# A hybrid backbone layer on one core: a list of small products on 32x32 tiles, and the products for an empty state left out

## The chip, the cores and the metric

One Trainium2 chip, one of its cores. The metric is the device time of one run of the kernel, in microseconds; less is better. Shares and rows of the profile are from one execution that the hardware profiler recorded.

## What is computed

One layer over 256 latent tokens and 256 context tokens, model width 2048, all in float32. Two token mixers stand side by side after one common projection: the first branch (RWKV-7, 16 heads of 64, worked as 8 pairs, scanned in both directions) and the second branch (gated DeltaNet, 8 heads of 128, in both directions). Their outputs are gated, merged and projected; a SwiGLU network of hidden width 5632 follows. The context tokens come first in each scan, from an empty state, and the state that they leave starts the scan of the latent tokens. The part that matters here, cut from the reference (the second branch; the kernel works the first branch in chunks with the same kind of triangular inverse):

```python
lmat = jnp.where(strict, jnp.einsum('nbhik,nbhjk->nbhij', kb, kc) * decay, 0.0)
sol = lax.linalg.triangular_solve(lmat, rhs, left_side=True, lower=True, unit_diagonal=True)
u, wk = sol[..., :dv], sol[..., dv:]
def step(s, inp):
    qk_i, u_i, w_i, qd_i, kt_i, gl_i = inp
    v_new = u_i - jnp.einsum('bhck,bhkv->bhcv', w_i, s)
    o = jnp.einsum('bhck,bhkv->bhcv', qd_i, s) + jnp.einsum('bhcj,bhjv->bhcv', qk_i, v_new)
    s = s * gl_i[..., None, None] + jnp.einsum('bhck,bhcv->bhkv', kt_i, v_new)
    return s, o
s0b = jnp.zeros((bsz, GDN_HEADS, GDN_HEAD_DIM, GDN_HEAD_DIM), jnp.float32)
```

## The kernel before

Large projections (`gemm`, and `products` in the middle stage) split each float32 operand into a high and a low part and take three matmuls per 128-row slice; ScalarE writes the high part of the weights, VectorE the low part (tiles `whi`, `wlo`, result `mm`). Three stages follow each other. Up to about 240 us the modulation vectors and the normalised input are made. From about 240 to 1300 us the two branches run, woven with the projections that they need. From there to the end come the merge, the output projection and the SwiGLU network, which are projections one after another.

The middle stage is written as generators (`prepare`, `grams`, `inverse`, `values`, `scan` per pair of the first branch; `features`, `tokens`, `decays`, `head_grams`, `head_inverse`, `head_scan` per head of the second; `products` for the projections). Each yields its next operation, or a list of matmuls, and class `Weave` puts all of them into one fixed order when the program is built. It keeps a clock for every engine from costs of its own (class `Lane`; a matmul with at most 64 rows and columns is charged by its rows and width), takes the operation that can start first by these clocks, and settles ties by the ranks in `RANK`. A list of matmuls is handed out in groups of 32, and another piece of work may come in between two groups. What the planner thinks an operation costs thus decides the order on every engine and on the DMA queues; what it really costs decides the time.

`invert` inverts the triangular blocks of 64x64 of a pair or head. For the first branch it is called once for a pair with `nu = 16` units of two 64x64 blocks each (32 blocks in all: 2 heads, 2 directions, 8 chunks), for the second branch once for a head with `nu = 8`. The 16x16 blocks on the diagonal are inverted by substitution on VectorE, after a round trip through DRAM that lays each block out along one partition. Then two steps of matmuls go from 16 to 32 and from 32 to 64. The step from 16 to 32 takes two lists of products, both into one PSUM tile (`pi`, seen as `pv`): the first list makes the product of the off-diagonal block with the inverse, on 32x32 tiles (`fours` names the 32x32 blocks); VectorE masks it into `Qm`; the second list multiplies the transposed inverse `Tx` by `Qm`; VectorE and ScalarE copy the result back into `T0`. In the second list, pairs (`nu = 16`) and heads (`nu = 8`) take different forms. In the trace the first list is `pi<-arena` (pairs) and the second `pi<-arena,Tx`.

In a head of the second branch, `tokens` scales the transposed keys into `keg` and `kta` for both directions and the four blocks of 128 tokens. `head_scan` multiplies `keg` by the inverse `tf` into `NW` (negated by ScalarE on its way out of PSUM), and then walks through the blocks in the order `gorder`, [2, 3, 0, 1] forward and [3, 2, 1, 0] backward: `NW` times the state `St` is subtracted from the values in every block but the first (the state is empty there), and `kta` times the new values makes the next state in every block but the last.

Most operations of the middle stage are issued from one helper, so they all carry its line, L147; in the rows they are told apart by the tiles.

Of the kernel before, what the change touches and what calls it, by code (L numbers as in the profile page):

```python
# [11 lines left out]
F32 = mybir.dt.float32  # L12
F32R = mybir.dt.float32r
AF = mybir.ActivationFunctionType
# [4 lines left out]
P = 128  # L19
# [264 lines left out]
def emit(ctx: ExitStack, tc, A, out, dbg=None):  # L284
# [6 lines left out]
    e, v, s = Lane(E, 0.0, 0.0, 0.0), Lane(V, 0.07, 0.00104, LAT["own"], 0.13), Lane(S, 0.09, 0.00086, LAT["own"], 0.165)  # L291
# [130 lines left out]
    with tc.tile_pool(name="p0", bufs=1) as p0, \  # L422
# [31 lines left out]
        ps = pst(pa, "pa")  # L454
# [9 lines left out]
        ps = pst(pa, "pa")  # L464
# [59 lines left out]
        for part in range(NE + 1):  # L524
            if part < NE:
                ps = pst(pmm, "mm")
# [48 lines left out]
    def invert(pool, Lt, parts, nu, which, full, fill):  # L575
# [7 lines left out]
        late = 0.0 if nu == 16 else 1.2  # L583
# [52 lines left out]
        for d in range(2):  # L636
            yield v.scalar_tensor_tensor(Qm[:, us[d]], pv[:, 0, us[d]], low16[:, d:d + 1],
                                         eye16[:, d].unsqueeze(1).to_broadcast([P, h2, 16]), ALU.mult, ALU.add)
        if nu == 16:
            yield [e.matmul(pv[64 * h:64 * h + 64, 1, u], Tx[64 * h:64 * h + 64, u, :], Qm[64 * h:64 * h + 64, u, :],  # L640
                            start=True, stop=True) for u in range(nu) for h in range(2)]
        else:
            yield [e.matmul(pv[r, 1, u], Tx[r, u, b:b + 32], Qm[r, u, :], start=True, stop=True) for h, u, b, r in fours]
        for h in range(2):
# [521 lines left out]
    gs = Shared()  # L1166
# [113 lines left out]
    def tokens(h):  # L1280
# [17 lines left out]
        for d in range(2):  # L1298
            col = 8 * d + h
            yield v.tensor_mul(keg[:, d], p4, egc[:, :, col:col + 1].to_broadcast([P, 4, P]))  # L1300
            yield v.tensor_mul(kta[:, d], p4, eta[:, :, col:col + 1].to_broadcast([P, 4, P]))
        weave.release(pab)
# [89 lines left out]
    def head_scan(h):  # L1392
# [9 lines left out]

        NW = gs.tile([P, 2, 4, P], F32, tag="NW", name="NW")
        for d in range(2):
            ps = yield psb
            yield [e.matmul(ps[:, P * b:P * b + P], keg[:, d, b, :], tf[:, 4 * d + b, :], start=True, stop=True) for b in range(4)]
            yield s.activation(NW[:, d].rearrange("p b c -> p (b c)"), ps, AF.Identity, scale=-1.0)
            weave.release(psb)
# [4 lines left out]
        for n in range(4):  # L1413
            bs = (gorder[0][n], gorder[1][n])
            ps = yield psb
            yield [e.matmul(ps[:, P * d:P * d + P], tf[:, 4 * d + bs[d], :], vt[:, bs[d], :], start=True, stop=n == 0) if i == 0 else
                   e.matmul(ps[:, P * d:P * d + P], NW[:, d, bs[d], :], St[:, d, :], start=False, stop=True)
                   for d in range(2) for i in range(1 + (n > 0))]
# [385 lines left out]
```

## Time and profile before

| | |
|---|---|
| time, median of 3 runs | 2226.66 us (2222.66 to 2231.06) |
| profiled execution, first to last instruction | 2220.3 us |
| TensorE busy | 2147.7 us (97%), 22780 matmuls |
| weight loads of TensorE | 1915.3 us (86%) |
| VectorE busy | 1554.6 us (70%) |
| ScalarE busy | 1063.0 us (48%) |
| GpSimd busy | 94.4 us (4%) |
| DMA | 435.13 MB, mean 196 GB/s |

Engines are named PE (TensorE's matmuls), PEld (its weight loads), DVE (VectorE), ACT (ScalarE), POOL (GpSimd) and SP (SyncE, which issues DMAs). Busy time is the union of what the engine had under way; matmuls overlap, so in a list of short ones the time from the list's start to the next operation's start is its price, not the length of one. A float32 matmul outside the split projections is recorded as two matmuls and two loads. "issue" in a wait means that the engine waited for nothing that the profile shows. Granted clock 1.00 is 2.4 GHz, 0.5 is 1.2 GHz; a mean between them is a mixture over the stretch.

### The profile page before, as it was taken

How to read it: one execution, taken by the hardware profiler on the slowest of the kernel's cores; microseconds unless marked ns; L12 is line 12 of the kernel's file. 1: busy time of each engine (PE TensorE's matmuls, PEld its weight loads, DVE VectorE, ACT ScalarE, POOL GpSimd, SP SyncE). 2: the span in 40 equal slices, each digit the busy share in tenths (PEclk: the TensorE clock that was granted, in tenths of full speed). 3: DMA queues.
4: the chain of work that ended last, by engine and by line, in shares of the span. 5: the costliest groups of instructions: out<-in, count | busy, mean ns of one | idle time of the engine just before them, and what ended most of it. 6: DMA issues, size and time to landing. Idle time of an engine off the chain costs nothing.

```text
span 2220.3 us, 54391 instructions
## 1 busy us (share of the span) xinstructions
PE 2147.7 (97%) x22780; PEld 1915.3 (86%) x22780; DVE 1554.6 (70%) x3244; ACT 1063.0 (48%) x1872; POOL 94.4 (4%) x171
## 2 busy tenths in 40 slices
PE   6998999999999999999999999999999999999998
PEld 4776688777778778878789899999999999999997
DVE  3457488778788668899998879956665665544454
ACT  3246555444555555545455465544444444444443
POOL 0000000000000011011110010100000000000000
PEclk8999999999999999999999999999999999999999
DMA  9965544344343446565667797927777776566665
GB/s 382 413 183 172 171 116 131 103 104 114 94 124 112 113 138 197 160 182 180 172 197 252 259 342 269 357 94 227 235 237 236 234 236 203 188 186 190 188 189 160
DMA packets 234484, 435.13 MB, mean 196 GB/s; under 512 B 115328, under 2 KB 129664, under 8 KB 229888
## 3 DMA queue, kind: packets, MB, share of 16 engines
q1 hardware_dynamic: 206304, 355.11, 50.9%
q0 software_dynamic: 14112, 51.39, 7.1%
q10 hardware_dynamic: 13824, 25.17, 3.4%
q8 instruction: 178, 2.92, 0.5%
q14 instruction: 66, 0.54, 0.1%
HBM read 405.76 MB, written 25.84 MB: 194 GB/s over the span
## 4 chain that ended last, share of the span: by engine, by line
issue 43%; PE 40%; DVE 8%; DMA 5%; ACT 2%; POOL 1%; SPq 0%; POOLq 0%; ACTq 0%; DVEq 0%
PE mm L147 19%; PE s L147 4%; PE pa L147 4%; DVE arena L147 3%; PE mm L380 2%; PE pi L147 2%; PE mm L382 2%; PE mm L381 2%; DVE wlo L147 2%; PE mm L475 1%; DVE aw L147 1%; DMA wraw<-w_low 1%; DMA wraw<-pa 1%; DMA aw<-ada_rest 1%; DMA arena<-scr 1%
## 5 line engine op out<-in xcount | busy, mean ns | idle before, releaser
L371 DVE TENSOR_TENSOR wlo<-wraw,whi 128x1024 fp32r<-128x1024 f32 x328 | 392.6, 1198 | 318.7 <-ACT whi L370 316.2
L370 ACT CAST whi<-wraw 128x1024 fp32r<-128x1024 f32 x328 | 336.6, 1028 | 457.8 <-PE mm L381 397.7
L147 PE MATMUL mm<-hxh,whi 128*128 128x256 f32 (+1 forms) x1376 | 465.6, 338 | 4.3 <-ACT whi L147 2.4
L147 PE MATMUL mm<-hxh,wlo 128*128 128x256 f32 (+1 forms) x1376 | 463.3, 337 | 4.6 <-DVE wlo L147 4.5
L147 PE MATMUL mm<-hxl,whi 128*128 128x256 f32 (+1 forms) x1376 | 462.4, 336 | 0.9 <-issue 0.9
L382 PE MATMUL mm<-hfh,wlo 128*128 128x256 f32 x1344 | 375.3, 279 | 0.2 <-DVE wlo L371 0.2
L380 PE MATMUL mm<-hfh,whi 128*128 128x256 f32 x1344 | 375.0, 279 | 0.0
L381 PE MATMUL mm<-hfl,whi 128*128 128x256 f32 x1344 | 375.0, 279 | 0.0
L147 PEld LDWEIGHTS mm<-hxh,wlo 128*128 128x128 f32 x1376 | 263.6, 192 | 31.5 <-DVE wlo L147 6.7
L147 PEld LDWEIGHTS mm<-hxh,whi 128*128 128x128 f32 x1376 | 263.4, 191 | 29.1 <-ACT whi L147 2.9
L147 PEld LDWEIGHTS mm<-hxl,whi 128*128 128x128 f32 x1376 | 263.3, 191 | 24.9 <-issue 4.2
L147 DVE TENSOR_TENSOR wlo<-wraw,whi 128x512 fp32r<-128x512 f32 x344 | 236.4, 689 | 50.8 <-ACT whi L147 48.4
L382 PEld LDWEIGHTS mm<-hfh,wlo 128*128 128x128 f32 x1344 | 252.8, 188 | 0.7 <-DVE wlo L371 0.6
L380 PEld LDWEIGHTS mm<-hfh,whi 128*128 128x128 f32 x1344 | 252.8, 188 | 0.0
L381 PEld LDWEIGHTS mm<-hfl,whi 128*128 128x128 f32 x1344 | 252.8, 188 | 0.0
L147 ACT CAST whi<-wraw 128x512 fp32r<-128x512 f32 x344 | 205.5, 617 | 85.0 <-PE mm L147 56.8
L147 DVE TENSOR_TENSOR arena<-arena 128x28 f32<-128x28 f32 (+13 forms) x538 | 131.4, 246 | 23.2 <-DMA arena<-scr 10.2
L380 PE MATMUL mm<-za,whi 128*128 128x256 f32 x512 | 142.9, 279 | 0.0
L381 PE MATMUL mm<-za,whi 128*128 128x256 f32 x512 | 142.7, 279 | 0.0
L382 PE MATMUL mm<-za,wlo 128*128 128x256 f32 x512 | 142.7, 279 | 0.0
L147 ACT ACTIVATE arena<-arena 128x512 f32<-128x512 f32 (+3 forms) x132 | 76.6, 593 | 45.6 <-DVE arena L147 33.9
L380 PEld LDWEIGHTS mm<-za,whi 128*128 128x128 f32 x512 | 96.3, 188 | 0.0
(325 smaller groups left out, 3892.7 us busy)
## 6 DMA issues: line engine op xcount, KB each, us to landing
wraw<-w SPq DMA_DIRECT2D x172, 512.0 KB, 4.2
wraw<-wgu SPq DMA_DIRECT2D x168, 512.0 KB, 4.6
aw<-ada_rest POOLq DMA_DIRECT2D x96, 512.0 KB, 5.4
aw<-ada_first SPq DMA_DIRECT2D x32, 1024.0 KB, 12.3
wraw<-wdn SPq DMA_DIRECT2D x64, 448.0 KB, 3.5
wraw<-wout SPq DMA_DIRECT2D x32, 512.0 KB, 6.8
aw<-ada_gt ACTq DMA_DIRECT2D x64, 256.0 KB, 5.0
wraw<-wdn SPq DMA_DIRECT2D x32, 512.0 KB, 3.6
```

The source lines that it names most:

```text
L147: return Op(self, cost, lambda: getattr(self.engine, name)(out, *a, **k), kind)
L370: S.copy(hi[:, c, :M], raw[:, c, :M])
L371: V.tensor_sub(lo[:, c, :M], raw[:, c, :M], hi[:, c, :M].bitcast(F32))
L380: E.matmul(ps, hi, Xh[:, k, :n], start=first and i == 0, stop=False)
L381: E.matmul(ps, hi, Xl[:, k, :n], start=False, stop=False)
L382: E.matmul(ps, lo, Xh[:, k, :n], start=False, stop=last and i == len(wt) - 1)
L475: E.matmul(ps[32 * g:32 * g + 32, 0:P], ckr[:, k].rearrange("p a b -> p (a b)"), aws[e, c][:, i, g], start=k == 0, stop=k == KT - 1)
```

## The change

Two edits in the middle stage. In `invert`, the pairs' second list takes the form that the heads' has: 64 products on 32x32 blocks in place of 32 products on 64x64 blocks. The off-diagonal 32x32 blocks, which the 64-row form multiplied along, are no longer read; the result that is copied back is the same. In the heads, the block that meets the empty state gets no `NW`: three products for a direction in place of four, `NW` holds three blocks in the order in which the scan takes them, and the negation covers 384 columns in place of 512. In `tokens`, for the backward direction the blocks of `keg` and `kta` that nobody reads are left out (block 3 of `keg`, block 0 of `kta`); for the forward direction the multiplies stay whole.

```diff
--- before.py
+++ after.py
@@ -636,11 +636,7 @@
         for d in range(2):
             yield v.scalar_tensor_tensor(Qm[:, us[d]], pv[:, 0, us[d]], low16[:, d:d + 1],
                                          eye16[:, d].unsqueeze(1).to_broadcast([P, h2, 16]), ALU.mult, ALU.add)
-        if nu == 16:
-            yield [e.matmul(pv[64 * h:64 * h + 64, 1, u], Tx[64 * h:64 * h + 64, u, :], Qm[64 * h:64 * h + 64, u, :],
-                            start=True, stop=True) for u in range(nu) for h in range(2)]
-        else:
-            yield [e.matmul(pv[r, 1, u], Tx[r, u, b:b + 32], Qm[r, u, :], start=True, stop=True) for h, u, b, r in fours]
+        yield [e.matmul(pv[r, 1, u], Tx[r, u, b:b + 32], Qm[r, u, :], start=True, stop=True) for h, u, b, r in fours]
         for h in range(2):
             yield [(s.copy if h else v.tensor_copy)(T0[r, us[d], b + 16 * d:b + 16 * d + 16], pv[r, 1, us[d]])
                    for d in range(2) for b in (0, 32) for r in (slice(64 * h + b, 64 * h + b + 32),)]
@@ -1297,8 +1293,9 @@
         p4 = ps.rearrange("p (b c) -> p b c", b=4)
         for d in range(2):
             col = 8 * d + h
-            yield v.tensor_mul(keg[:, d], p4, egc[:, :, col:col + 1].to_broadcast([P, 4, P]))
-            yield v.tensor_mul(kta[:, d], p4, eta[:, :, col:col + 1].to_broadcast([P, 4, P]))
+            late, soon = (slice(0, 4 - d), slice(d, 4))
+            yield v.tensor_mul(keg[:, d, late], p4[:, late], egc[:, late, col:col + 1].to_broadcast([P, 4 - d, P]))
+            yield v.tensor_mul(kta[:, d, soon], p4[:, soon], eta[:, soon, col:col + 1].to_broadcast([P, 4 - d, P]))
         weave.release(pab)
         weave.ready("tok", h)
 
@@ -1400,11 +1397,12 @@
             yield "out", NPAIR - 1
         tf, keg, kta, vt, Qe, PT = (o[n] for n in ("tf", "keg", "kta", "vt", "Qe", "PT"))
 
-        NW = gs.tile([P, 2, 4, P], F32, tag="NW", name="NW")
+        NW = gs.tile([P, 2, 3, P], F32, tag="NW", name="NW")
         for d in range(2):
             ps = yield psb
-            yield [e.matmul(ps[:, P * b:P * b + P], keg[:, d, b, :], tf[:, 4 * d + b, :], start=True, stop=True) for b in range(4)]
-            yield s.activation(NW[:, d].rearrange("p b c -> p (b c)"), ps, AF.Identity, scale=-1.0)
+            yield [e.matmul(ps[:, P * i:P * i + P], keg[:, d, b, :], tf[:, 4 * d + b, :], start=True, stop=True)
+                   for i, b in enumerate(gorder[d][1:])]
+            yield s.activation(NW[:, d].rearrange("p b c -> p (b c)"), ps[:, :3 * P], AF.Identity, scale=-1.0)
             weave.release(psb)
         if h:
             yield "gout", h - 1
@@ -1414,7 +1412,7 @@
             bs = (gorder[0][n], gorder[1][n])
             ps = yield psb
             yield [e.matmul(ps[:, P * d:P * d + P], tf[:, 4 * d + bs[d], :], vt[:, bs[d], :], start=True, stop=n == 0) if i == 0 else
-                   e.matmul(ps[:, P * d:P * d + P], NW[:, d, bs[d], :], St[:, d, :], start=False, stop=True)
+                   e.matmul(ps[:, P * d:P * d + P], NW[:, d, n - 1, :], St[:, d, :], start=False, stop=True)
                    for d in range(2) for i in range(1 + (n > 0))]
             Vn = gs.tile([P, 2, P], F32, tag="Vn", name="Vn")
             for d in range(2):
```

## Rows read from the trace of the kernel before

**Rows 1.** the page's busy time, share of the span and instructions of each engine
```profile
PE 2147.7 (97%) x22780; PEld 1915.3 (86%) x22780; DVE 1554.6 (70%) x3244; ACT 1063.0 (48%) x1872; POOL 94.4 (4%) x171
```

**Rows 2.** busy us in stretches of 50 us: start:end length, engines, clock, DMA
```profile
500.00:550.00 50.00, 49.78 (x669) 38.98 (x667) 44.44 (x115) 24.44 (x57) 2.31 (x6) 1.00 0.44 112
...
1100.00:1150.00 50.00, 49.98 (x532) 43.93 (x532) 48.69 (x130) 26.39 (x54) 4.88 (x8) 1.00 0.67 199
```

**Rows 3.** whom TensorE waited for, 240 to 800 us: total, times, longest
```profile
PE pi L147 <- issue: 7.5, 6, 2.8
```

**Rows 4.** TensorE's timeline, sixth inversion: start us, us, operation, count, idle before
```profile
626.50 1.26 PE L147 MATMUL pi<-arena 32*32 32x16 f32 x128
627.69 0.50 PE L147 MATMUL mm<-hxh,whi 128*128 128x512 f32 x1
...
629.51 2.08 PE L147 MATMUL pi<-arena,Tx 64*64 64x16 f32 x64
631.53 0.50 PE L147 MATMUL mm<-hxl,whi 128*128 128x512 f32 x1
```

**Rows 5.** the page's DMA queues: packets, MB, share of 16 engines
```profile
q8 instruction: 178, 2.92, 0.5%
```

**Rows 6.** busy us (x instructions), from one stall's end to the next
```profile
250.91:341.05 90.14, 89.77 (x1144) 73.75 (x1143) 73.42 (x175) 47.68 (x109) 2.76 (x8) 0.96 0.41 119
341.05:410.25 69.21, 66.00 (x1017) 53.51 (x1018) 57.40 (x144) 31.44 (x73) 3.50 (x6) 0.98 0.43 117
```

**Rows 7.** the same, from one instruction packet to the next, second, third, sixth inversion
```profile
337.04:341.05 4.01, 3.74 (x153) 2.94 (x140) 4.01 (x9) 1.51 (x4) 0.45 (x2) 1.00 0.62 210
404.39:410.25 5.86, 3.04 (x144) 2.33 (x137) 3.00 (x7) 0.00 (x0) 0.00 (x0) 1.00 0.64 206
...
626.95:630.88 3.94, 3.94 (x149) 3.33 (x140) 3.88 (x11) 0.00 (x0) 0.00 (x0) 1.00 0.70 207
```

**Rows 8.** TensorE's timeline, third inversion
```profile
406.32 1.11 PE L147 MATMUL pi<-arena 32*32 32x16 f32 x110
410.26 0.33 PE L147 MATMUL pi<-arena 32*32 32x16 f32 x18 [2.83 <-issue]
...
411.98 3.60 PE L147 MATMUL pi<-arena,Tx 64*64 64x16 f32 x64
415.51 1.22 PE L147 MATMUL pa<-Y,C 128*128 128x256 f32 x2
```

**Rows 9.** TensorE's timeline, fourth inversion
```profile
484.41 1.26 PE L147 MATMUL pi<-arena 32*32 32x16 f32 x128
...
487.45 1.22 PE L147 MATMUL pi<-arena,Tx 64*64 64x16 f32 x35
490.41 1.65 PE L147 MATMUL pi<-arena,Tx 64*64 64x16 f32 x29 [1.74 <-issue]
```

**Rows 10.** busy us and granted clock around the second, third and sixth inversion
```profile
340.00:350.00 10.00, 9.81 (x178) 7.65 (x178) 7.68 (x15) 3.36 (x8) 0.00 (x0) 0.83 0.28 90
410.00:420.00 10.00, 9.74 (x102) 8.08 (x102) 6.03 (x15) 5.81 (x16) 0.00 (x0) 0.66 0.11 34
...
628.00:634.00 6.00, 6.00 (x84) 5.01 (x83) 5.33 (x17) 1.45 (x5) 0.00 (x0) 1.00 0.44 137
```

**Rows 11.** TensorE's timeline, a head's second list at the lower clock
```profile
1083.53 1.04 PE L147 MATMUL pi<-arena,Tx 32*32 32x16 f32 x64
1084.49 0.71 PE L147 MATMUL pa<-arena 128*128 128x128 f32 x4
```

**Rows 12.** whom TensorE's weight loads waited for, 800 to 1260 us
```profile
PEld pi L147 <- DVE arena L147: 8.1, 11, 1.7
```

**Rows 13.** the chain that ended last, first head's NW products
```profile
887.90 0.89 PE s L147 x8
```

**Rows 14.** instructions by line and shape: busy us, mean ns, idle before
```profile
L147 DVE TENSOR_TENSOR arena<-pa,C 128x256 f32<-128x256 f32 x32 | 13.3, 417 | 5.9 <-PE pa L147 5.4
...
L147 DVE TENSOR_TENSOR keg<-pa,egc 128x512 f32<-128x512 f32 x16 | 10.8, 676 | 1.4 <-PE pa L147 1.4
```

## The prediction, made before the changed kernel ran

> **What bounds the kernel now.** I read the page's busy shares first, then the engines in stretches of 50 us. TensorE is busy for 97% of the span [rows 1]; in the stage of the first branch's heads (about 250 to 800 us) and in that of the second branch's (800 to 1260 us), where the two edits lie, it is all but full, and VectorE comes close only in the second [rows 2]. Then I read whom TensorE waited for between 240 and 800 us: the one large wait is "pi <- issue", 7.5 us in six pieces [rows 3]. So a microsecond of TensorE's own time there is nearly one of the kernel's, and its one large stall sits in the edited lists. Last, TensorE's timeline around an inversion.
>
> An undisturbed inversion, the sixth, looks like [rows 4]: the first list, 128 matmuls on 32x32 tiles (64 products, each recorded as two matmuls), runs from 626.50 to 627.69, which is 1.19 us, 9.3 ns each. Projections pass while VectorE masks the result. The second list, 64 matmuls on 64x64 tiles (32 products), runs from 629.51 to 631.53: 2.02 us, 31 ns each. The small form goes through three times as fast per matmul.
>
> **What the "issue" stalls are.** I counted instructions. Queue q8 carries them: 178 packets, 2.92 MB, so 16.4 KB each [rows 5]. TensorE has 22780 matmuls and 22780 loads [rows 1]: 256 to a packet. Between the end of one stall and the end of the next lie 2287 and, for the next pair, 2035 matmuls and loads [rows 6], 9 and 8 times 256 less 17 and 13 (semaphore instructions are not counted there). So TensorE stalls just where a new packet begins: it has used up 256 instructions before the next ones came. Going back 256 from each stall, the time from entering one packet to having the next is 4.01 us at the least and 5.86 us at the most in the inversions that stalled, and 3.94 us in the sixth, which did not stall [rows 7]. I take 5 us. Whoever issues 256 instructions faster than that waits; the first list is 256 instructions in 1.2 us. The third inversion stalls for 2.83 us in its first list [rows 8], the fourth for 1.74 us in its second [rows 9].
>
> **The change part by part.**
>
> *Second list.* Eight inversions each replace 64 matmuls on 64x64 tiles by 128 on 32x32 tiles, with the same 16 columns. The first list has that form, count and width, so its price is taken: 1.19 us for 2.02 us [rows 4], 0.83 us saved; seven times, 5.8 us. In the third inversion the list took 3.53 us [rows 8]: the granted clock over 410 to 420 us was 0.66 [rows 10], a part of it at 1.2 GHz. A 32x32 list of 64 there takes 0.96 us [rows 11], so 128 take 1.9 us, and 1.6 us is saved. Together 7.4 us; bounds 5.8 (the third gains nothing) and 9.0 (two more lists fall at 1.2 GHz, 0.8 us more each). It is TensorE's own time, on the path; the evictions behind it, on VectorE and ScalarE, only come earlier.
>
> Here a rule of the Trainium skill speaks against the change. The rows show 9.3 ns from one 32x32 matmul to the next [rows 4]. "TensorEngine Tiling (Array Packing)", section Performance Considerations, has every matmul carry an overhead of some 60 cycles however narrow it is, and warns against tiling where a dimension is already small; by that (an estimate: 60 cycles at 2.4 GHz, 25 ns) 64 more matmuls would cost 1.6 us an inversion, 12.8 us in all. The trace does not agree: its 9.3 ns lies far below.
>
> *Instructions.* 64 more matmuls bring 64 more loads: the second list issues 256 instructions in place of 128. The lists start 3.0 us apart in [rows 4] and in [rows 9]. The first list always holds one packet boundary. Now, the instruction 256 further on lies in the second list only if that boundary is in the first half of the first list; else the second list is over and slow 512-column matmuls are running. After the change it lies in the second list nearly always, and is reached as long after the first boundary as the lists are apart, 2.9 us. With 5 us to a packet that is a stall of 2.1 us. I let one in five escape (a boundary at the start of the first list, fetched while slow matmuls still run), and leave out two inversions of eight whose lists are far apart, as in [rows 8], 5.7 us: 6 x 2.1 x 0.8 = 10.1 us. Today's are 4.7 us (7.5 less the 2.83 of a first list). Added: 5.4 us. Bounds: 0 (packets come as in the sixth) and 12 (all eight stall by 2.1 us). In a stall only TensorE stands still; queued behind it are the projections, and what evicts them waits too.
>
> *Clock.* The granted clock falls around some inversions, to 0.83 of full over 340 to 350 us at the second, to 0.66 at the third, and stays at 1.00 at the sixth [rows 10]. In [rows 8] it was down after an issue stall between short matmuls. With shorter lists and longer stalls I see no net sign: 0. One such fall costs what the second's does, 0.17 of 10 us, 1.7 us; three falls more or two less give bounds of +5 and -3.5 us.
>
> *Order.* The order of all instructions between 240 and 1300 us comes from a planner in the file that uses its own costs. It charges the old second list 32 x (0.01 + 0.00075 x 16) = 0.70 us and the new one 64 x (0.01 + 0.00037 x 16) = 1.02 us. So the plan shifts by 0.3 us at each inversion, and everything after the first may interleave anew: casts, weight loads on SP's queue, evictions. No row prices that. TensorE's loads wait for VectorE in the second stage 8.1 us in eleven pieces [rows 12]; such waits may come or go. I take 0, bounds 5 us either way.
>
> *Heads of the second branch.* Per head and direction one 128x128x128 product (two matmuls) goes: four matmuls a head. Eight take 0.89 us [rows 13], 0.11 us each: 0.45 us a head, 3.6 us in all. On VectorE one keg and one kta multiply of each head shrink from 512 to 384 columns; 512 cost 676 ns and 256, also from PSUM, 417 [rows 14], so 0.13 us each, 2.1 us in 16; ScalarE's negation shrinks by a quarter. ScalarE idles enough to hide its part; TensorE's 3.6 us count. Bounds: 0 (VectorE, at 48.69 of 50 us [rows 2], holds the pace there) and 5 (its own part helps as well).
>
> **Sum.** -7.4 + 5.4 + 0 + 0 - 3.6 = -5.6 us. The profiled span is 2220.3 us, the median of the runs 2226.66; I leave the 6.4 us between them. 2226.66 - 5.6 = 2221 us. What is late next is TensorE as before, with its own instructions inside the inversions.
>
> **Rivals.** *Packets come in time.* The 5.4 us fall away: -11.0 us, 2215.7; with the better ends of lists and heads, -14, 2212.7. For it: the sixth inversion's 3.94 us [rows 7]. Against: the ones with 4.01 to 5.86. Chance 0.20.
>
> *Starved lists,* slower than before. All eight second lists stall by 2.1 us (16.8 in place of 4.7: +12.1), and the clock falls at three inversions more than now (+5); lists and heads give -11.0: +6.1, 2232.8. It decides from the point where stalls and falls add over 11 us, 1.4 us an inversion. For it: [rows 8] has stall and lower clock together. Against: the sixth has neither. Chance 0.13.
>
> *No faster per matmul.* If something else than the tile's size holds this list (its operands, its bank), a matmul still costs 31 ns: 128 take 4.0 us, +2.0 x 8 = +15.8, heads -3.6: +12.2, 2238.9. The change would then not do what it says. Against: the first list, with the same bank and width [rows 4]. Chance 0.04.
>
> *A new order outweighs the edit,* by some 10 us around the forecast: 2211 or 2231. Chance 0.11, half each way. The forecast itself: 0.52.
>
> **How the numbers follow.** A measurement of this kernel tells about 0.5% from no change, 11.1 us: faster is below 2215.5, slower above 2237.8. Faster: a little over half of the first rival (0.13), half of the new order (0.05), the low edge of the forecast (0.06): 0.24. Slower: the no-faster case (0.03), the upper end of starved lists and new order (0.07): 0.10. The rest, 0.66, can't be told from no change. The range for 8 in 10 reaches from the better half of the first rival, 2209 with the order's bound, to the starved lists, 2234.
>
> **What would show it.** In the profile after: "pi<-arena,Tx" as 128 matmuls on 32x32 tiles in about 1.2 us outside stalls, eight times; "pi <- issue" up from 7.5 to about 13 us; stalls still multiples of 256 instructions apart; "s<-TF,keg" with 96 matmuls. Wrong would be: issue stalls that stay or shrink, a list of 2 us without a stall, or a stage whose length moves against its lists.

## The result and the profile after

The changed kernel takes 2237.82 us (median of 5 runs, 2232.97 to 2239.14), the kernel before, run beside it, 2226.19 us: a ratio of 1.0045, 95% interval 1.0024 to 1.0067. It is 11.6 us slower, 10 us by the ratio. The forecast was 5.6 us faster, and the time lies above the range's upper end of 2234; it stays just within the 0.5% that was called no change. The profiled execution takes 2234.9 us, 14.6 more than that of before.

The page of the changed kernel, its span, its busy line and the queue of the instructions:

```profile
span 2234.9 us, 55358 instructions
...
PE 2146.3 (96%) x23260; PEld 1915.0 (86%) x23260; DVE 1557.2 (70%) x3244; ACT 1061.1 (47%) x1872; POOL 97.1 (4%) x171
...
q8 instruction: 182, 2.98, 0.6%
```

Against [rows 1] TensorE has 480 more matmuls (8 x 64 in the lists, less 32 in the heads), as the edit says, and nearly the same busy time. What grew is the time in which it is not busy: 2234.9 less 2146.3 is 88.6 us; before it was 72.6.

The lists themselves cost what was expected of them. TensorE's timeline of the changed kernel (start us, us, operation, count, idle before) at the fifth and the seventh inversion, both second lists on 32x32 tiles:

```profile
536.87 1.26 PE L147 MATMUL pi<-arena 32*32 32x16 f32 x128
540.48 1.23 PE L147 MATMUL pi<-arena,Tx 32*32 32x16 f32 x125
544.54 0.23 PE L147 MATMUL pi<-arena,Tx 32*32 32x16 f32 x3 [2.83 <-issue]
...
684.77 1.26 PE L147 MATMUL pi<-arena 32*32 32x16 f32 x128
687.87 1.59 PE L147 MATMUL pi<-arena,Tx 32*32 32x16 f32 x128
```

125 of them take 1.23 us, where 64 on 64x64 tiles took 2.02 us in [rows 4]; and the fifth stalls for 2.83 us just before its last three. In the changed kernel each of the eight second lists but the last has a wait in it, of 0.15 us (the seventh) to 2.83 us (the fifth); without it they take 1.1 to 1.5 us, and the last, at 1.2 GHz, 1.9. TensorE's waits from 240 to 800 us (total, times, longest), the row that answers to [rows 3] and the same wait in another tile:

```profile
PE pi L147 <- issue: 9.3, 7, 2.8
PE pa L147 <- issue: 1.3, 1, 1.3
```

Now the stages. Start:end and length, busy us of TensorE, its loads, VectorE, ScalarE and GpSimd (with instructions), granted clock, DMA. The bounds are the same events in both kernels: the first pair's first list, the last pair's first list, the first head's first list, the first gate product (`oah`) and the first output product (`mh`). Before:

```profile
246.80:754.60 507.80, 497.94 (x7297) 401.95 (x7298) 413.44 (x1038) 263.08 (x613) 15.47 (x41) 0.97 0.41 112
754.60:871.60 117.00, 116.37 (x1225) 97.32 (x1224) 87.36 (x202) 64.48 (x125) 11.63 (x15) 1.00 0.51 160
871.60:1263.10 391.50, 378.98 (x4336) 329.12 (x4335) 351.94 (x919) 198.13 (x400) 43.66 (x69) 0.99 0.63 193
1263.10:1368.50 105.40, 100.28 (x830) 98.23 (x829) 84.72 (x134) 59.58 (x82) 9.30 (x17) 1.00 0.88 315
```

After:

```profile
248.50:746.00 497.50, 487.02 (x7801) 397.50 (x7800) 418.08 (x1041) 263.21 (x613) 15.81 (x41) 0.99 0.43 117
746.00:874.00 128.00, 118.02 (x1203) 95.29 (x1204) 82.88 (x188) 62.46 (x123) 11.30 (x14) 0.91 0.41 126
874.00:1272.00 398.00, 379.56 (x4250) 330.53 (x4249) 348.88 (x920) 194.81 (x395) 46.45 (x69) 0.97 0.62 191
1272.00:1380.70 108.70, 105.50 (x911) 103.14 (x912) 89.16 (x144) 62.78 (x90) 8.72 (x16) 0.97 0.87 311
```

In the stage of the first branch's inversions, where the lists lie, the changed kernel is 10.3 us shorter. That is not the lists' doing: in before_neworder, a run that is told of below, the second lists are still on 64x64 tiles, the order is the changed kernel's, and the stretch is 11.6 us shorter than before, with 56 more matmuls in it:

```profile
245.60:741.80 496.20, 490.46 (x7353) 402.13 (x7352) 418.40 (x1041) 263.61 (x613) 15.83 (x41) 0.99 0.43 117
```

Nor does one execution settle a difference of some 5 us in such a stretch. In heads_oldorder, also told of below, every engine has the same instructions there in the same order as before, and the stretch takes 5.5 us less:

```profile
248.70:751.00 502.30, 493.00 (x7294) 397.97 (x7293) 413.65 (x1038) 262.66 (x614) 14.26 (x41) 0.98 0.41 113
```

The changed kernel gives 11.0 us back between the last inversion and the first head, where TensorE idles 10.0 us (0.6 before) and the clock is 0.91 (1.00 before); 6.5 more among the heads, 3.3 in the stage behind them. With 1.7 us ahead of the first list and 2.4 in the long last stage this makes the 14.6.

A clock of 0.91 over 128 us is a mean of stretches at 2.4 GHz (1.00) and at 1.2 GHz (0.50): 0.09 x 2 x 128 = 23 us were at the lower level. Over the whole span the mean clock is 0.983 before and 0.977 after, 75 and 103 us at 1.2 GHz. Where TensorE is the bound, each such microsecond does half a microsecond's work, so the 27 us more cost about 14.

What TensorE waited for in those 128 us:

```profile
PE mm L147 <- ACT whi L147: 4.2, 2, 2.8
PE mm L147 <- DVE wlo L147: 2.8, 2, 2.3
PE pi L147 <- issue: 1.7, 1, 1.7
PE pa L147 <- issue: 1.3, 1, 1.3
```

7.0 of the 10.0 us are waits for split weights, of which before had 0.2 us in that stretch. They come with the order: before_neworder, with the work of before, has 7.0 us of them too (742 to 865 us):

```profile
PE mm L147 <- ACT whi L147: 4.0, 2, 2.6
PE mm L147 <- DVE wlo L147: 3.0, 3, 2.3
```

One of them in the changed kernel, in the timeline of all engines:

```profile
819.25 1.14 ACT L147 CAST whi<-wraw 128x512 fp32r<-128x512 f32 x2
...
819.92 0.50 PE L147 MATMUL mm<-hxh,whi 128*128 128x512 f32 x1 [1.41 <-ACT whi L147]
...
820.35 0.74 DVE L147 SCALAR_TENSOR_TENSOR arena<-mm,PR,arena 128x510 f32<-128x510 f32 x1
821.01 0.68 DVE L147 TENSOR_TENSOR kta<-pa,eta 128x512 f32<-128x512 f32 x1
821.60 0.74 DVE L147 SCALAR_TENSOR_TENSOR arena<-mm,PR,arena 128x510 f32<-128x510 f32 x1
822.26 0.68 DVE L147 TENSOR_TENSOR wlo<-wraw,whi 128x512 fp32r<-128x512 f32 x1
...
823.00 0.80 PE L147 MATMUL mm<-hxh,wlo 128*128 128x512 f32 x1 [2.35 <-DVE wlo L147]
```

and the same place in stretches:

```profile
810.00:818.00 8.00, 8.00 (x36) 5.83 (x35) 2.61 (x7) 4.09 (x10) 2.66 (x4) 1.00 0.58 198
818.00:829.00 11.00, 7.25 (x24) 5.57 (x23) 9.13 (x18) 4.64 (x9) 0.53 (x1) 0.69 0.43 131
```

The high parts were written from 819.25 on, 0.57 us each; the low part of them stands behind three other multiplies in VectorE's order and is issued at 822.26. TensorE has nothing else next in its own order, waits 1.41 and 2.35 us, and runs at 1.2 GHz for a while (0.69 over the stretch). VectorE is busy for 9.1 of the 11 us; what TensorE needs next stands late in its order. That order is the planner's, and the planner was given new charges.

### The profile page after: what moved, and what is told of

It reads as the page before. It is cut to its first block, busy times and chain, and to the rows that moved or that the text cites. A ratio compares the mean times of both kernels' runs of the same rounds, so it can differ in the third digit from the quotient of the medians.

```text
span 2234.9 us, 55358 instructions
## 1 busy us (share of the span) xinstructions
PE 2146.3 (96%) x23260; PEld 1915.0 (86%) x23260; DVE 1557.2 (70%) x3244; ACT 1061.1 (47%) x1872; POOL 97.1 (4%) x171
## 5 line engine op out<-in xcount | busy, mean ns | idle before, releaser
L147 DVE TENSOR_TENSOR arena<-arena 128x512 f32<-128x512 f32 (+13 forms) x538 | 132.6, 248 | 20.0 <-DMA arena<-scr 5.1
```

The source lines that it names most:

```text
L147: return Op(self, cost, lambda: getattr(self.engine, name)(out, *a, **k), kind)
```

## The experiments

Two ways to hold things apart. In *the old order* the edited operations are issued, but the planner is charged what it was charged before, so that in the middle stage every engine's sequence is that of the kernel before except for the edited operations themselves. In *the new order* it is the other way round. The operations of the merge and of what follows are written behind the planner's stage, and the planner does not set their order. By the traces the runs in the old order keep the sequences of before up to 1268 us; behind that some differ from it in a few places. before_neworder has the changed kernel's sequence on TensorE, VectorE and ScalarE up to 1281 us (SyncE's DMAs differ in four places); behind that, in the merge, its order is a third one. All runs, each beside the kernel before, whose median was 2223.9 to 2226.2 in the five sessions ("not busy" is the profiled span less TensorE's busy time; the last two columns are of the profiled execution):

| run | us | ratio to before (95%) | not busy us | mean clock |
|---|---|---|---|---|
| before | 2226.19 | | 72.6 | 0.983 |
| changed kernel | 2237.82 | 1.0045 (1.0024 to 1.0067) | 88.6 | 0.977 |
| both_oldorder | 2228.38 | 1.0014 (0.9997 to 1.0032) | 81.5 | 0.982 |
| before_neworder | 2242.92 | 1.0078 (1.0055 to 1.0101) | 88.7 | 0.979 |
| list_only | 2225.56 | 1.0002 (0.9984 to 1.0019) | 85.2 | 0.984 |
| heads_only | 2251.77 | 1.0105 (1.0078 to 1.0132) | 92.9 | 0.977 |
| heads_oldorder | 2224.18 | 0.9999 (0.9984 to 1.0015) | 73.8 | 0.984 |
| list_oldorder | 2229.87 | 1.0021 (1.0003 to 1.0038) | 85.2 | 0.982 |
| after_headsold | 2229.70 | 1.0021 (1.0002 to 1.0040) | 87.2 | 0.984 |
| before_turn | 2261.04 | 1.0160 (1.0133 to 1.0187) | 92.4 | 0.980 |
| before_hop | 2266.46 | 1.0182 (1.0151 to 1.0212) | 106.4 | 0.975 |
| before_own | 2265.40 | 1.0176 (1.0136 to 1.0216) | 96.6 | 0.975 |
| after_own | 2244.42 | 1.0085 (1.0055 to 1.0114) | 95.9 | 0.980 |
| list_twice | 2264.24 | 1.0177 (1.0153 to 1.0200) | 98.5 | 0.978 |
| list_half | 2219.56 | 0.9978 (0.9963 to 0.9992) | 79.7 | 0.985 |
| first_big | 2216.18 | 0.9965 (0.9941 to 0.9988) | 69.2 | 0.990 |
| first_wide | 2222.53 | 0.9982 (0.9967 to 0.9998) | 77.0 | 0.992 |
| first_wide_heads | 2219.30 | 0.9970 (0.9956 to 0.9984) | 76.1 | 0.988 |

### Work and order apart

Both edits, charged as before (the heads' operations likewise, through a helper that sets an operation's charge back):

```diff
-            yield [e.matmul(pv[64 * h:64 * h + 64, 1, u], Tx[64 * h:64 * h + 64, u, :], Qm[64 * h:64 * h + 64, u, :],
+        ops = [e.matmul(pv[r, 1, u], Tx[r, u, b:b + 32], Qm[r, u, :], start=True, stop=True) for h, u, b, r in fours]
+        yield paired(ops) if nu == 16 else ops
```

(`paired` makes 32 operations of two products each, charged 0.022 us like the 64-row products.)

> Both edits of the change, but the planner charges the edited operations as it charged the old ones (32 entries of two products each at the old list's cost and kind, a fourth empty entry in each list of three NW products, old costs for the shortened multiplies and the negation), so that the order of the woven stage is that of the kernel before. Theory A, the new interleaving costs the time and the edited work itself is a gain: TensorE's waits on the heads' casts are as in the kernel before, the granted clock falls in the heads twice as before (10 us), and the time is 2215 to 2222 us, ratio 0.995 to 0.998. Theory B, the work itself costs it (twice the instructions in the second lists, so longer fetch stalls, and a lower clock after them): 'pi <- issue' rises from 7.5 to 13 us or more, the clock falls at more inversions, and the time is 2230 to 2240 us.

Measured: 2228.38 us, some 3 us above before and between what A (2215 to 2222) and B (2230 to 2240) gave; issue waits between 240 and 800 us are 12.3 us, close to B's sign. The same work in the changed kernel's order has the ratio 1.0045 in place of 1.0014: the order makes some 7 us of it, between 1 and 13 by the two intervals (an estimate). The work of the kernel before, in the order that the changed kernel's charges give:

```diff
+            yield [x for o in ops for x in (Op(e, 0.01 + 0.00037 * 16, o.call, (32, 32)), Op(e, 0.01 + 0.00037 * 16, lambda: None, (32, 32)))]
...
+            yield charged(v.tensor_mul(keg[:, d], p4, egc[:, :, col:col + 1].to_broadcast([P, 4, P])), 512, 512 - 128 * d)
```

> The work of the kernel before (32 products on 64x64 tiles, four NW blocks, full multiplies), but the planner charges it as it charges the changed kernel's, so that the woven stage has the changed kernel's order. Theory A: slower than the changed kernel by what the edited work saves, 5 to 11 us: 2243 to 2249 us. Theory B: about the time of the kernel before, 2222 to 2230 us, since the work that costs the time is gone.

Measured: 2242.92 us, a ratio of 1.0078, at A's lower end. Not one operation more or less, and the kernel is 17 us slower (0.0078 x 2224): an order alone can cost more than the changed kernel loses. But it is not the price of the changed kernel's order. Of the 20.5 us that the profiled execution takes more, 14.6 lie in the stage behind the heads, 120.0 us against 105.4 before and 108.7 in the changed kernel, where the order is a third one:

```profile
1267.50:1387.50 120.00, 108.32 (x915) 105.54 (x916) 92.47 (x146) 64.91 (x91) 9.79 (x18) 0.96 0.81 288
```

From the first list to the first head the two do have the same order. There before_neworder takes 618.6 us and the changed kernel 625.5 (before 624.8, heads_oldorder with the same work 621.1). So there the order itself loses nothing, and the edited lists lose some 7 us in it, by one execution each: issue waits are 10.6 us against 4.2, and 38 us against 24 are at 1.2 GHz from 240 to 875 us. Among the heads it is the other way: 403.3 us in before_neworder, 398.0 in the changed kernel, 391.5 before. Each edit alone, with its own charges: list_only is the first hunk of the change, heads_only the other three.

> The second list on 32x32 tiles alone, ordered by the planner with its own charge for it; the heads as before. Theory A: another order, whose cost or gain is not foreseen, within some 15 us of 2222 us. Theory B: the list is what costs: 2235 to 2242 us, the heads' edit having given 3 to 4 us back in the changed kernel.

> The heads' edit alone, planned as it comes; the second list on 64x64 tiles. The first branch has the order of the kernel before until the heads begin to be woven in. Theory A: an order of its own among the heads, within some 10 us of 2223 us. Theory B: 2222 to 2223 us, the edit's 3.6 us less.

Measured: 2225.56 and 2251.77; the second lies above what either theory gave for it. The list's edit is neutral with its own charges, the heads' costs 23 us (0.0105 x 2224), though it only leaves work out. The list's order is not harmless either. In list_only, from the first pair's list to the last pair's, and from there to the first head's:

```profile
248.80:742.10 493.30, 483.85 (x7805) 394.70 (x7807) 417.83 (x1041) 263.79 (x613) 15.83 (x41) 1.00 0.43 118
742.10:872.20 130.10, 119.11 (x1229) 96.81 (x1228) 87.60 (x201) 64.00 (x125) 12.47 (x15) 0.95 0.42 133
```

14.5 us are won in the first stretch and 13.1 lost in the second, on waits for `whi` and `wlo` (7.4 us) as in the changed kernel.

### Which edit, which charge

> The heads' edit alone, with the planner still charged the old cost for the shortened multiplies, the shortened negation and the product left out, so that all instructions come in the order of the kernel before. Theory A (the new order is what costs; the edited work itself is worth what the rows say): TensorE's own 0.45 us a head come out, 2220 to 2222.5 us beside 2224. Theory B (the heads' edit itself disturbs the second stage, by VectorE's or ScalarE's results coming at other times): 2230 to 2252, as the edit gave with its own plan (2251.8).

Measured: 2224.18 us, ratio 0.9999, some 2 us above A's range and far from B's. The 23 us of heads_only were the order's alone; the work left out is worth 1 us here, at most 3.6 by the interval. The NW products are 12 in place of 16 a head, and from the first head's to the last head's TensorE's busy time falls from 360.7 to 357.2 us, the 0.5 us a head that the prediction took; the stretch itself falls from 372.9 to 371.7 only.

> Both edits in full; the planner is charged the new cost for the second list, and the old cost for the heads' multiplies, negation and product. Theory A (the heads' new charges bring the order that costs): 2221 to 2226, the list's edit alone (2225.6) less 0 to 3.6 us for the heads. Theory D (the two edits together cost, whatever the order): 2234 to 2242, as the changed kernel.

Measured: 2229.70 us, between the two theories' numbers and 8 us under the changed kernel. With the heads charged as before most of the loss seems gone, but the intervals of the two (1.0002 to 1.0040 and 1.0024 to 1.0067) overlap.

> The list's edit alone (second list as 64 products on 32x32 tiles), with the planner charged the old cost for it, so that all instructions come in the order of the kernel before. Theory A (the edit saves TensorE 6 to 7 us and its longer stalls at packet boundaries and what is late next give 4 to 9 us back): 2221 to 2227 beside 2224, TensorE's busy time down by about 6 us and its waits up by as much. Theory L (in a held order the whole saving stays): 2216 to 2219.

Measured: 2229.87 us, above what A gave and 11 us above L: in a held order the list's edit costs 0.7 to 8.5 us. A part of the saving goes at the last inversion, which ran undisturbed before. TensorE's timeline there (the view ends at 758 us; 92 matmuls of the list stand behind the stall), and the granted clock behind it:

```profile
752.59 1.32 PE L147 MATMUL pi<-arena 32*32 32x16 f32 x128
...
755.36 0.49 PE L147 MATMUL pi<-arena,Tx 32*32 32x16 f32 x36
757.94 0.25 PE L147 MATMUL pi<-arena,Tx 32*32 32x16 f32 x5 [2.09 <-issue]
```

```profile
752.60:767.90 15.30, 13.21 (x290) 10.95 (x289) 5.90 (x18) 4.51 (x16) 1.05 (x1) 0.67 0.18 65
752.60:875.30 122.70, 120.04 (x1289) 100.17 (x1288) 87.49 (x202) 64.47 (x125) 11.58 (x15) 0.96 0.49 152
```

The new instructions bring a stall of 2.09 us in the second list, as the prediction had it, and behind it 10 us at 1.2 GHz (0.33 x 2 x 15.3). From the last list to the first head it takes 122.7 us, before 117.0. Up to that list it took 502.3 us against 507.8, but so did heads_oldorder with the lists of before, so that nothing shows the lists to have won there.

### How much an order is worth

The work of the kernel before, untouched, with one constant of the planner moved by 2 to 6%:

```diff
-LAT = dict(dma=2.04, hop=0.255, own=0.092, grp=32, cg=4, turn=0.17)
+LAT = dict(dma=2.04, hop=0.255, own=0.092, grp=32, cg=4, turn=0.18)
```

`turn` becomes 0.18 in before_turn; in before_hop it is `hop`, 0.26, and in before_own `own`, 0.095. after_own sets `own` to 0.095 in the changed kernel.

> All work is that of the kernel before; only one constant of the planner is changed, the time it puts in for a change of tile form on TensorE, 0.17 to 0.18 us. It plans another order of the same instructions. Theory A (the order alone moves the time by more than the edits are worth): off by 5 us or more from 2224, either way, up to 25 slower; the difference sits among the second branch's heads and in the stage behind them, with TensorE waits on casts and VectorE and a lower granted clock there. Theory C (only the particular charges for the heads give a bad order; neighbouring plans are alike): 2221 to 2227.

> All work is that of the kernel before; one other constant of the planner is changed, the time it puts in from one engine's result to another engine's start, 0.255 to 0.26 us. Theory A (plans of the same work spread by tens of us, and the plan of the kernel before is a good one among them): 2230 to 2262, with more TensorE waits and more low clock than before. Theory C (the turn's plan was an outlier): 2222 to 2229.

> All work is that of the kernel before; a third constant of the planner is changed, the time between two dependent instructions of VectorE, ScalarE or GpSimd, 0.092 to 0.095 us. Theory A (plans of the same work spread by tens of us, and the plan of the kernel before is a good one among them): 2230 to 2262. Theory C: 2222 to 2229.

> The changed kernel, both edits with their new charges, with the same third constant changed, 0.092 to 0.095 us: another order of the changed kernel's work. Theory A (the changed kernel's 2238 is one draw from a spread that the order makes, not the price of the edits): anywhere from 2215 to 2262, off from 2238 by 5 us or more. Theory D (the edits themselves cost 12 to 14 us): 2234 to 2242.

Measured: 2261.04, 2266.46 and 2265.40 us, 35 to 41 us slower than before for the same work, and 2244.42 for the changed kernel's. Theory A holds for the three, and its upper ends (25 us, and 2262) were too low (in before_turn 12 of the 32 us of the profiled execution lie ahead of the heads, where A did not put them); the particular charges of the heads are not special. For after_own the interval, 1.0055 to 1.0114, reaches the changed kernel's 1.0067, so that this run decides little. Four other orders of the work of before are 17 to 41 us slower, the two of the changed kernel 12 and 19. Only with the planner's constants and the heads' charges left alone did new orders come out near the old one (list_only, after_headsold). By these runs the order of the kernel before is a good one among worse.

Busy line and largest waits (240 to 1420 us) of before_hop:

```profile
PE 2160.9 (95%) x22780; PEld 1930.3 (85%) x22780; DVE 1561.0 (69%) x3244; ACT 1062.8 (47%) x1872; POOL 95.0 (4%) x171
```

```profile
PE pi L147 <- DVE arena L147: 10.4, 13, 2.0
PE mm L147 <- DVE wlo L147: 7.7, 4, 4.5
PE pi L147 <- ACT T L147: 4.7, 2, 2.4
PE pa L147 <- DVE kta L147: 4.2, 2, 3.3
PE pi L147 <- DVE T L147: 3.7, 3, 2.9
```

No one wait is the cause: they are many, spread over VectorE and ScalarE, and the clock falls behind them. TensorE is not busy for 33.8 us more than before, and 113 us are at 1.2 GHz against 75, worth 19 more; together 53 us, for a span longer by 47.0. For before_neworder the same sum gives 16.1 + 9.3 = 25 us for 20.5. The account closes to about 6 us. One place comes back: in before_neworder, heads_only, before_turn, before_hop and before_own the stage behind the heads takes 113 to 124 us, in all runs in the old order 103 to 106.

### Instructions in a burst

The prediction's mechanism itself, that TensorE runs out of instructions, was tested in the old order. The second list issued twice:

```diff
+        yield [Op(o.lane, o.cost, twofold(o.call), o.kind) for o in paired(ops)] if nu == 16 else ops
```

> Only the second list of the first branch's eight inversions is changed: 64 products on 32x32 tiles, and the whole list is issued a second time, rewriting the same values, 512 instructions in place of 128. The planner is charged as before, so the order is that of the kernel before. Theory F (instructions come in packets of 256, 4 to 5.9 us from entering one to having the next): each inversion crosses two or three packet boundaries within 768 instructions, the gaps at the boundaries grow from about 14 us (list issued once) to 35 to 50 us, and the time to 2248 to 2265. Theory P (the lists cost only TensorE's own time, the gaps are something else): 128 more matmuls of 9.3 ns in each of eight, +9.5 us over the list issued once, 2233 to 2237, and the gaps stay at about 14 us.

Measured: 2264.24 us, 34 us above the list issued once. Its waits from 240 to 800 us and its first branch:

```profile
PE pi L147 <- issue: 30.1, 16, 2.8
```

```profile
246.60:783.10 536.50, 506.85 (x8641) 409.17 (x8642) 413.69 (x1038) 262.79 (x614) 14.35 (x41) 0.96 0.39 106
```

That is theory F, with stalls somewhat under its 35 to 50 us: 16 of them, 30.1 us, where list_oldorder has 8 with 10.1. 128 more matmuls at 9.3 ns are 9.5 us in all, the stalls 20 us more.

Half of the second list, with no more instructions than the list of before (the inverses are other values):

```diff
+        ops = [e.matmul(pv[r, 1, u], Tx[r, u, b:b + 32], Qm[r, u, :], start=True, stop=True) for h, u, b, r in fours if nu != 16 or b == 0]
```

> The second list issues only half of its products, 32 on 32x32 tiles, so 128 instructions as in the kernel before, in a quarter to a third of the time; the evictions behind it read the half that is there. The inverses of the first branch are therefore other values; only the time is read. The planner is charged as before, so the order is that of the kernel before. Theory F (in a held order the list's saving is taken by the 128 more instructions: longer stalls at packet boundaries, and the lower clock behind them): with no more instructions than before the saving of 1.4 us in each of eight inversions stays, 2210 to 2218, with issue waits of 5 to 9 us. Theory V (the saving is taken by what is late next, VectorE's masks and evictions, whatever the instructions): 2222 to 2227, with the waits on VectorE up by 8 to 12 us.

Measured: 2219.56 us, 5 us less than before (1.8 to 8.2), issue waits 7.7 us. That is between F and V: without further instructions some of the saving stays, though not the 11 us that the rows of the lists promise.

The other way round, the first list of each inversion as 32 products on 64x64 tiles (again other values): 128 instructions fewer, 6.6 us more of TensorE's own time.

```diff
+            ops = [e.matmul(pv[64 * h:64 * h + 64, 0, u], Lt(h, u), T0[64 * h:64 * h + 64, u, 16 * (u // h2):16 * (u // h2) + 16],
+                            start=True, stop=True) for u in range(nu) for h in range(2)]
```

> The second list is that of the kernel before; the first list of the first branch's inversions goes out as 32 products on 64x64 tiles (64 matmuls, 128 instructions) in place of 64 on 32x32 tiles (128 matmuls, 256 instructions). A product then takes in more of the matrix than it should, so the inverses are other values; only the time is read. The planner is charged as before, so the order is that of the kernel before. Theory F (half the instructions of the lists mean hardly a stall at a packet boundary, and fewer falls of the clock): TensorE's own time rises by 0.83 us in each of eight, 6.6 us, issue waits fall from 7.5 us to 0 to 2, low clock between 246 and 755 us falls to under half of 27 us, and the time is 2212 to 2224. Theory P (stalls and clock falls have other causes): +6.6 us, 2229 to 2233.

Measured: 2216.18 us, 8 us faster than before (2.7 to 13.1), with not one issue wait between 240 and 800 us, and its first branch in

```profile
247.60:741.20 493.60, 490.57 (x6847) 397.65 (x6846) 414.01 (x1038) 262.69 (x613) 14.24 (x41) 1.00 0.43 115
```

14.2 us less than before (8.7 less than heads_oldorder), at a clock of 1.00 in place of 0.97. The slower form of the list is the faster one for the kernel.

### A version that beats both

The same with the right values: both blocks' columns go through the 64-row tile, and VectorE picks the right ones with four masked multiplies in place of two. Charged as before.

```diff
+            ops = [e.matmul(wide[64 * h:64 * h + 64, u], Lt(h, u), cols[u // h2][64 * h:64 * h + 64, u % h2],
+                            start=True, stop=True) for u in range(nu) for h in range(2)]
...
+                one = v.scalar_tensor_tensor(Qm[:, us[d]], wide[:, us[d], 0], lowb[:, d:d + 1], eye, ALU.mult, ALU.add)
+                two = v.scalar_tensor_tensor(Qm[:, us[d]], wide[:, us[d], 1], lowb[:, 2 + d:3 + d], Qm[:, us[d]], ALU.mult, ALU.add)
```

> The second list is that of the kernel before. The first list of the first branch's inversions goes out as 32 products on 64x64 tiles, each with both blocks' 16 columns (64 matmuls of 32 columns, 128 instructions in place of 256); VectorE picks the right block with four masked multiplies in place of two. It computes the whole. The planner is charged as before, so the order is that of the kernel before. Theory F (fewer instructions in the lists are worth more than TensorE's faster small form): issue waits of 0 to 2 us, 2214 to 2222 beside 2225. Theory V (the two further multiplies, some 0.25 us each on the chain of each inversion, are waited for): 2222 to 2230.

> As the run before, and the heads' edit of the changed kernel too (product left out, shorter multiplies and negation), all of it charged as before, in the order of the kernel before. Theory F: another 0 to 3 us less, 2212 to 2221, faster than both kernels. Theory V: 2221 to 2229.

Measured: 2222.53 us alone (ratio 0.9967 to 0.9998) and 2219.30 us with the heads' edit (0.9956 to 0.9984), which is faster than both kernels of this case; the two do not differ from each other by more than their intervals. first_wide's first inversion and its first branch:

```profile
245.73 2.05 PE L149 MATMUL pi<-arena 64*64 64x32 f32 x64
249.27 2.04 PE L149 MATMUL pi<-arena,Tx 64*64 64x16 f32 x64 [0.35 <-DVE arena L149]
```

```profile
245.70:743.80 498.10, 491.18 (x6847) 397.08 (x6846) 417.92 (x1052) 263.11 (x614) 15.47 (x41) 1.00 0.42 114
```

No issue wait, clock 1.00, 9.7 us less than before. The time lies at the border of the two theories. The masks are waited for, 2.9 us in eight pieces (0.3 before), which is theory V's part.

## Why the prediction was wrong

Two steps failed: the order, priced at 0, and the sum of the edits' own work, -5.6 us, of which little or nothing is left even in the old order.

**The lists: right in their price.** 125 matmuls in 1.23 us are the 1.2 us for a whole list that it asked for. That the first branch's stretch is 10.3 us shorter does not bear it out: with the old lists it was 11.6 shorter in before_neworder. By the 60 cycles a matmul that the Trainium skill's "TensorEngine Tiling (Array Packing)", Performance Considerations, gives, the edit would have cost TensorE 12.8 us (the prediction's estimate); the trace still shows some 10 ns a matmul.

**Instructions: right in kind, and in size as far as it can be told.** It asked for +5.4 us between bounds of 0 and 12. Between 240 and 800 us issue waits went from 7.5 us in the old order to 10.1 (list_oldorder) and 12.3 (both_oldorder), and in the changed kernel's order from 4.2 (before_neworder) to 10.6. The same lists in the same order gave 5.4 in heads_oldorder, so that 2 us are within the scatter. Between stalls of the changed kernel lie again multiples of 256 instructions less a few uncounted ones, as in [rows 6], for example from 544.54 to 618.83 us 1018 + 1019 = 2037, 8 x 256 less 11. list_twice and first_big drive the waits up to 30.1 us and down to 0 in the same order, with 384 instructions more and 128 fewer an inversion.

**Order: the first step that failed.** "I take 0, bounds 5 us either way", it said, and "No row prices that". The changed kernel's order makes some 7 us (1 to 13) of its loss, as both_oldorder shows; other orders of unchanged work cost 17 us (before_neworder) and 35 to 41. The step saw that everything behind the first inversion may interleave anew, and still priced it by one existing wait of 8.1 us [rows 12]. It also drew the bounds evenly. But rows of before are rows of one order, in which the stretch from the last inversion to the first head had 0.6 us of idle time and a clock of 1.00: there was little to gain there, and a new order could lose. The rival "A new order outweighs the edit" was the one that came nearest. It had 0.11, half of it on the wrong side, and a size of 10 where the orders of unchanged work gave 17 to 41.

**Clock: right in the lists, wrong where it counted.** In the old order the falls in the first branch hardly change (clock 0.97 before, 0.98 in both_oldorder and list_oldorder), so the 0 held there; but one moved to the last inversion, where list_oldorder loses 5 us. What it missed is that a new order's waits have falls of their own with them, far from the edited lists: 103 us at 1.2 GHz in place of 75, some 14 us, where the bound was 5.

**Heads: right on TensorE, little or nothing of it kept.** 3.6 us of TensorE's own time were taken; 3.5 went, as 360.7 less 357.2 us shows. The time fell by 1.4 us, with an interval from 3.6 less to 3.3 more. The bound of 0 was the likelier end. TensorE's waits for VectorE from 868 to 1263 us went from 10.1 to 12.8 us, which fits VectorE holding the pace, but rests on one execution each. The shrunken multiplies take 0.55 us in place of 0.68, the 0.13 that was estimated.

**The sum in the old order: the second step that failed.** Without any effect of the order the prediction says -5.6 us, and both_oldorder measures +3 (0.7 less to 7 more). TensorE's busy time fell by 7.3 us in the profiled execution, not by 11.0, and its time not busy rose by 8.9, not by 5.4; 4.8 of that are issue waits from 240 to 800 us. Why the rest came is only partly shown: the stall and the clock behind the last inversion are (122.7 us in list_oldorder, where before takes 117.0 and heads_oldorder 118.8); the rest, some microseconds, stays open. Stalls and lower clock against a small gain is the mechanism of the rival "Starved lists" (+6.1 us), which had 0.13. That the saving can be kept when nothing is added to the bursts is shown by list_half, for less than half of it.

**What stays open.** Why the other orders are worse by 12 to 41 us is not settled further than this: the waits are many and small, the clock is lower with them, and in the five runs named there 8 to 19 us of the profiled difference lie in the stage behind the heads. Whether a planner that knew the packets' boundaries and the clock would find better orders was not tried.

## What to carry to other kernels

If a program puts its own instructions in order by modelled costs, then an edit changes the order of everything behind it; measure the edit with the old charges and the old work with the new ones before believing either, and move one constant a little to see how far an order alone carries the time. Count the instructions of a burst and not only its time: here the form with half as many instructions and 1.7 times TensorE's own time (2.02 us for 1.19) was the faster one. Count the clock behind a wait, too: here one of 2.09 us had 10 us at 1.2 GHz behind it, worth 5. And do not credit an edit with a stretch of the trace that also got a new order, or with less than what two executions of the same work differ by, here 5 us.

## What the hardware showed

- The more TensorE stalls, the longer it runs at the lower clock. In the first branch the mean clock is 0.96 with 30.1 us of issue waits (list_twice), 0.97 with 7.5 (before) and 1.00 with none (first_big, first_wide). The Trainium skill's "TensorE: Matmul & The Clock Gate", section "HAM oscillation — how this bites in real kernels", tells of a kernel whose short bursts, parted by waits for DMA, run cold one after the other. The trace agrees in kind, with a wait for instructions and waits for other engines in the place of DMA's. But not every fall has a stall ahead of it: first_big is at 1.2 GHz for 3.4 us from 408.2 us, heads_oldorder for 3.4 us from 757.4, behind two lists of short matmuls with no wait of TensorE over 0.2 us in the 6 us before. How much of the falls the short matmuls themselves make is not shown.
- A matmul on a 64x64 tile costs the same with 32 columns as with 16: 64 matmuls of 32 columns go through in 2.05 us, of 16 columns in 2.04 (first_wide), 32 ns each; on 32x32 tiles a matmul takes 10.
- Leaving out work made the kernel 23 us slower (heads_only); in the old order the same edit made no difference that its interval shows (heads_oldorder, 3.6 us less to 3.3 more).
